# A list-scheduled recurrent scan on one Trainium2 core: loads on ScalarE's queue, state scaling on ScalarE, a fourth common bank, and new estimates

## The chip, the core and the metric

The kernel is one program on one core of a Trainium2 chip. Its engines are TensorE (PE, with its weight loads as PEld), VectorE (DVE), ScalarE (ACT), GpSimd (POOL) and SyncE (SP), which here only issues DMAs. Each runs its own instructions in order and they meet through semaphores. The metric is the device time of one execution in microseconds (us), lower is better. TensorE's clock has two levels, 1.2 and 2.4 GHz; the profile shows the granted clock as a share of the upper one.

## The reference

The model is a four-layer encoder on 528 tokens (16 meta tokens and 512 real ones) of 1024 features: latent attention (MLA) in layers 0 and 3, an RWKV-7 mixer in layer 1, a gated linear recurrence in layer 2, and a convolutional gated FFN behind each. The change is about the RWKV-7 mixer, 16 heads of 64 features in two directions:

```python
def _wkv7_scan(r, w, a, b, k, v, reverse):
    def step(S, inp):
        r_t, w_t, a_t, b_t, k_t, v_t = inp
        sa = jnp.einsum('bhvk,bhk->bhv', S, a_t)
        S = S * w_t[:, :, None, :] + sa[..., None] * b_t[:, :, None, :] + v_t[..., None] * k_t[:, :, None, :]
        return S, jnp.einsum('bhvk,bhk->bhv', S, r_t)
    ...
# in _rwkv7_mixer, for d in range(2):
    kd = kf * (1.0 + (a - 1.0) * k_a_h)
    ys.append(_wkv7_scan(rf, decay, -kk, kk * a, kd, vf, reverse=(d == 1)))
    bonuses.append(jnp.sum(rf * kd * r_k_h, axis=-1, keepdims=True) * vf)
```

Around it stand low-rank maps for decay, rate and gate, a normalisation of each head's output, and the output projection.

## The kernel before

The scan is computed in windows of 64 tokens. Eight pairs of heads times two directions make 16 chains; both heads of a pair lie side by side in the 128 partitions (64 each), so most matmuls are 64x64 and come in twos. What one chain i needs is written as Python generators that yield one operation at a time (`rwkv_scan`, from line 1362):

- `pair` loads r, k and v of a head pair (tiles `in_r`, `in_k`, `in_v`) from DRAM; `values` turns v.
- `stage_a` loads the second low-rank weights (`w2`), makes decay and rate, then the products `bk` and `xr`, and with matmuls `ps<-xr,bk` the masked matrices `am` (DVE).
- `inverses` inverts 16x16 diagonal blocks: SP sends blocks of `am` to DRAM (`sc<-am`) and loads them back one block per partition (`bu<-sc`); POOL does 15 elimination steps of two operations each (`dtmp<-bu,dt` and `dt<-dt,dtmp`); ACT copies the transpose (`dt<-dt`); SP sends it out and back (`sd<-dt`, `dc<-sd`, `xt<-sd`).
- `stage_b` builds the whole window inverse from it: DVE makes `dd<-dc`, then four products in a row, `rb<-dd,am`, `rb<-dd,nn` and twice `rb<-xt,nn`, each evicted by DVE before the next, and last `xa`.
- `chain` runs the nine windows one after another. In each, `ch<-s,xa` is copied by DVE to `u`, `ch<-u,tb` follows, and DVE's scalar_tensor_tensor makes the new state `s` from it and from `sp`, the old state times the decay. Before, `sp` is a POOL operation (line 1704). Chain i starts only when chain i-1 has ended.
- `bonus` and `post` finish a head pair; `post` loads the gate's weights (also a `w2` tile).

The order of all instructions is found at build time by the list scheduler `Streams`. `Op` estimates an operation's cost (and, for a DMA, a time `after` until the data are there); `LATENCY` adds a delay between engines; at each turn the operation that could start first by these estimates is emitted. Dependencies are kept on the chip by semaphores; a wrong estimate therefore only gives another order. The buffers set what may be ahead: three `am`, two `dc`, and a common set of PSUM banks (`ps`: three of the eight; two `ch`, one `rb`, one `yp`, one `idle`) that are taken and given back. Where the estimate leaves TensorE idle by over 150 ns and its estimated work of late is low, `fill` emits matmuls of 256 columns that nobody reads (fillers, "idle" in the rows). All operations of the scheduler are emitted at line 218, so rows are told apart by tiles. The MLA layers use the same class.

Of the kernel before, what the change touches and what calls it, by code (L numbers as in the profile page):

```python
# [48 lines left out]
GAP = 150.0  # L49
# [56 lines left out]
class Op:  # L106
    __slots__ = ("eng", "fn", "args", "kw", "outs", "ins", "cost", "work", "after", "mode")

    def __init__(self, eng, fn, name, args, kw):
        self.eng, self.fn, self.args, self.kw = eng, fn, args, kw  # L110
        aps = [x for x in list(args) + list(kw.values()) if hasattr(x, "tensor")]
        out = kw.get("out", args[0] if args else None)
        self.outs = [out] + ([kw["accum_out"]] if kw.get("accum_out") is not None else [])
        self.ins = [x for x in aps if all(x is not y for y in self.outs)]
        n = max([int(np.prod(x.shape[1:])) for x in aps if x is out or eng != "pe"] + [1])
        if eng == "pe":
            lhsT = kw.get("lhsT", args[1] if len(args) > 1 else None)
            m = lhsT.shape[-1]
            rows = lhsT.shape[0] / 128
            tile = lambda x: 32 if x <= 32 else 64 if x <= 64 else 128  # L120
            self.mode = tile(lhsT.shape[0]), tile(m)
            if lhsT.dtype == F32R:
                self.cost, self.work = max(2 * m, n) / 2.2, n * rows
            elif name == "transpose":
                self.cost, self.work = 2 * lhsT.shape[0] / 2.3, 2 * lhsT.shape[0] * rows
            else:
                self.cost, self.work = 4 * max(n, m / 2) * (0.56 if self.mode == (64, 64) else 0.35 if m <= 32 else 1.0) / 2.3, 4 * n * rows
        else:
            fixed, each = {"dve": (75, 0.5 if name == "tensor_scalar" else 1.04), "act": (50 if name == "copy" else 240 if kw.get("accum_out") is not None else 100, 0.835),
                           "pool": (140, 2.1), "dma": (475, 0)}[eng]  # L130
            self.cost = fixed + each * n
        self.after = 650 + 4 * out.shape[0] * n / 360 if eng == "dma" else 0.0


class Eng:
# [8 lines left out]
class Streams:  # L144
# [132 lines left out]
    def fill(self, start):  # L277

        t = self.free.get("pe", 0.0)
        self.did(t, 0.0)  # L280
        while start - t > GAP and self.work < NEED:
            n = max(64, min(256, int((start - t) * 2.4 * WARM))) // 2 * 2
            self.warm(n)
            t += n / 2.4
            self.did(t, n)
            self.mode = (128, 128)
        self.free["pe"] = t
# [38 lines left out]
class Kern:  # L326
# [1034 lines left out]
    def rwkv_scan(self, es, hid, rkv, yall):  # L1361
# [11 lines left out]
        def bank(name):  # L1373
            return sch.named(pp.tile([128, 512], F32, name=name, tag=name), name, 1)

        for kind, n in (("ps", 3), ("ch", 2), ("rb", 1), ("yp", 1)):
            for j in range(n):
                sch.slot(kind, lambda name=f"{kind}{j}": bank(name))
        sch.slot("sq", lambda: tl([128, T], "sq"))

        idle, dense = pp.tile([128, 512], F32, name="idle"), hid["w", 0]
        cst = cp.tile([128, a["rw_const"].shape[1]], F32, name="rwcst")
        nc.sync.dma_start(cst, a["rw_const"])
        mask = [cst[:, 128 * d:128 * d + 128] for d in range(2)]
# [82 lines left out]
        def pair(hp, P):  # L1467
            if hp >= 2:
                yield wait(f"bonus{hp - 2}")
            for n, name in ((2, "v"), (0, "r")):  # L1470
                P[name] = tl([128, T], "in_" + name, 2)
                yield dq.dma_start(P[name], rkv[n, hp])
            if hp >= 2:
                yield wait(f"front{2 * hp - 3}")
            P["k"] = tl([128, T], "in_k", 2)
            yield dq.dma_start(P["k"], rkv[1, hp])
            yield spawn(f"values{hp}", values(hp, P), prio("values", 2 * hp))
            kk = P["kk"] = tl([128, T], "kkh", 2)
            yield ve.tensor_scalar(out=kk, in0=P["k"], scalar1=self.p("rw_k_k", hp), scalar2=None, op0=ALU.mult)
            sq = yield take("sq")  # L1480
            yield ac.activation(out=sq, in_=kk, func=AF.Square)
            yield from over_norm(kk, sq, dict(scalar1=1e-24, scalar2=None, op0=ALU.max), dict(scalar1=0.5, scalar2=None, op0=ALU.mult))
            yield give(sq)
# [21 lines left out]
        def stage_a(i, hp, d, P, U):  # L1505
            if i:
                yield wait(f"front{i - 1}")
            if d == 0:
                raw = tl([128, 512], "w2")
                yield dq.dma_start(raw, a["rw_2"][hp, :, 0:512])  # L1510
                P["w2"] = tl([128, 512], "w2hi", 1, F32R), tl([128, 512], "w2lo", 1, F32R)
                yield from split(*P["w2"], raw)
            whi, wlo = P["w2"]
# [165 lines left out]
        def chain(i, hp, d, P, U):  # L1679
# [14 lines left out]
            for w, after in zip(order, order[1:] + [None]):  # L1694
# [5 lines left out]
                if after is not None:  # L1700
                    p1 = pc[:, w:w + 1]
                    if S is not None:
                        sp = tl([128, 64], "sp", 2)
                        yield po.tensor_tensor(out=sp, in0=S, in1=p1.to_broadcast([128, 64]), op=ALU.mult)
                    ps = yield take("ch")
                    yield from both(ps[:, 0:64], tb[:, 1, w], v[:, w], True, False)
                yield ve.tensor_copy(u[:, w], pu[:, 0:64])
# [42 lines left out]
        def post(hp, P):  # L1750
            yield wait(f"c{2 * hp + 1}", f"bonus{hp}", *([f"post{hp - 1}"] if hp else []))
            y = yall[:, hp]
            raw = tl([128, 512], "w2")[:, 0:256]
            yield dq.dma_start(raw, a["rw_2"][hp, :, 512:768])
            whi, wlo = tl([128, 256], "g2hi", 1, F32R), tl([128, 256], "g2lo", 1, F32R)
            yield from split(whi, wlo, raw)
            yield ac.copy(wlo[0:64, 128:256], whi[0:64, 128:256].bitcast(F32))
# [18 lines left out]
        for hp in range(KD):  # L1776
# [6 lines left out]
                sch.add(f"a{i}", stage_a(i, hp, d, P, U), prio("a", i))  # L1783
            sch.add(f"bonus{hp}", bonus(hp, P), prio("bonus", 2 * hp))
            sch.add(f"post{hp}", post(hp, P), prio("post", 2 * hp))
        sch.warm = lambda n: nc.tensor.matmul(idle[:, 0:n], lhsT=dense[:, 0:128], rhs=dense[:, 0:n], start=True, stop=True)
        with tc.manual_schedule():
            sch.run()
        if DEBUG:
# [144 lines left out]
```

## Time and profile before

| | us |
|---|---|
| median of three runs | 3481.4 (3481.07 to 3485.17) |
| profiled execution | 3473.31 |
| its span | 3471.5 |
| scan, from the first filler to the last DVE add of a chain | 992.6 to 1543.1 |
| ends of chains 4, 6, 8, 10 and 12 (copy of `yp`) | 1217.6, 1282.3, 1345.3, 1411.6, 1478.9 |

Over the span PE is busy 93%, DVE 78%, ACT 48% and POOL 27%. The steady part of the scan is best read between 1060 and 1480 us. There a matmul's busy time includes its way through the array, so two matmuls in a row overlap, and a busy PE isn't one that starts matmuls as fast as it could.

### The profile page before, as it was taken

Reading aid. Unit: us, or ns where it says so; the run is one execution under the profiler, and the core shown is the slowest. Engines: PE = TensorE matmul, PEld = TensorE weight load, DVE = VectorE, ACT = ScalarE, POOL = GpSimd, SP = SyncE. Lnnn points to the kernel's source line nnn. Section 1 sums busy time; section 2 is a strip of 40 time slices with the busy share of each in tenths; the row PEclk is TensorE's granted clock in tenths of the full one; section 3 lists DMA queues with packets and bytes.
Section 4 is the critical chain, followed back from the end, with each engine's and each line's share of the span. In section 5 each row is a group of like instructions: output and inputs, shape, how many; then the busy total and the mean of one; then the engine's idle time right before and its main releaser. Section 6 shows DMA issues by size and latency. Waiting matters only on the chain.

```text
span 3471.5 us, 77910 instructions
## 1 busy us (share of the span) xinstructions
PE 3216.4 (93%) x32057; PEld 3099.1 (89%) x32057; DVE 2701.7 (78%) x5006; ACT 1673.0 (48%) x3139; POOL 936.7 (27%) x1406
## 2 busy tenths in 40 slices
PE   7999999997988988879999988989999899989998
PEld 7899899996977878869999988989999799989998
DVE  6877789979336767657898788789886777788987
ACT  6665454433333333224544468654444666554443
POOL 0000143422016555433443200044331000034431
PEclk9999999998989999989999999999999999999999
DMA  2001223322322112113323222222322011112322
GB/s 84 34 33 40 84 71 104 99 87 88 136 69 50 35 40 45 25 42 102 98 95 107 80 73 74 80 73 88 106 86 83 21 38 35 65 64 83 101 93 72
DMA packets 157717, 250.07 MB, mean 72 GB/s; under 512 B 78736, under 2 KB 88112, under 8 KB 157232
## 3 DMA queue, kind: packets, MB, share of 16 engines
q1 hardware_dynamic: 157360, 245.08, 22.4%
q8 instruction: 252, 4.13, 0.5%
q14 instruction: 105, 0.86, 0.1%
HBM read 227.93 MB, written 17.10 MB: 71 GB/s over the span
## 4 chain that ended last, share of the span: by engine, by line
PE 47%; DVE 10%; ACT 6%; issue 2%; POOL 2%; DMA 2%; SPq 0%; DVEq 0%; ACTq 0%; POOLq 0%
PE bank L422 11%; PE bank L421 11%; PE bank L420 11%; PE pj L218 4%; PE ps L218 2%; PE s L218 1%; PE ch L218 1%; PE rb L218 1%; PE yp L218 1%; PE mm L420 1%; PE mm L421 1%; PE mm L422 1%; POOL dt L218 1%; ACT wv L218 1%; ACT th L1227 1%
## 5 line engine op out<-in xcount | busy, mean ns | idle before, releaser
L421 PE MATMUL bank<-xlo,whi 128*128 128x264 f32 x2272 | 655.7, 290 | 18.7 <-DVE xlo L562 10.9
L422 PE MATMUL bank<-xhi,wlo 128*128 128x264 f32 x2272 | 651.2, 289 | 12.4 <-DVE wlo L409 12.3
L420 PE MATMUL bank<-xhi,whi 128*128 128x264 f32 x2272 | 646.6, 289 | 15.4 <-ACT whi L408 13.8
L421 PEld LDWEIGHTS bank<-xlo,whi 128*128 128x128 f32 x2272 | 437.0, 192 | 26.1 <-DVE xlo L562 14.8
L420 PEld LDWEIGHTS bank<-xhi,whi 128*128 128x128 f32 x2272 | 432.7, 192 | 17.5 <-ACT whi L408 14.6
L422 PEld LDWEIGHTS bank<-xhi,wlo 128*128 128x128 f32 x2272 | 435.3, 192 | 14.4 <-DVE wlo L409 14.4
L422 PE MATMUL bank<-phi,wlo 128*128 128x264 f32 x1408 | 402.2, 286 | 0.0
L421 PE MATMUL bank<-plo,whi 128*128 128x264 f32 x1408 | 400.3, 284 | 0.0
L420 PE MATMUL bank<-phi,whi 128*128 128x264 f32 x1408 | 400.3, 284 | 0.0
L409 DVE TENSOR_TENSOR wlo<-wraw,whi 128x1024 fp32r<-128x1024 f32 (+1 forms) x234 | 262.8, 1125 | 116.0 <-ACT whi L408 115.8
L408 ACT CAST whi<-wraw 128x1024 fp32r<-128x1024 f32 (+1 forms) x234 | 222.4, 952 | 199.4 <-PE bank L421 157.8
L575 DVE TENSOR_TENSOR wlo<-wraw,whi 128x1024 fp32r<-128x1024 f32 (+1 forms) x216 | 286.3, 1326 | 29.7 <-ACT whi L574 28.1
L420 PEld LDWEIGHTS bank<-phi,whi 128*128 128x128 f32 x1408 | 265.4, 188 | 0.0
L422 PEld LDWEIGHTS bank<-phi,wlo 128*128 128x128 f32 x1408 | 264.9, 188 | 0.0
L421 PEld LDWEIGHTS bank<-plo,whi 128*128 128x128 f32 x1408 | 264.7, 188 | 0.0
L574 ACT CAST whi<-wraw 128x1024 fp32r<-128x1024 f32 (+1 forms) x216 | 195.2, 904 | 124.2 <-PE bank L421 72.4
L422 PE MATMUL bank<-thi,wlo 128*128 128x264 f32 x864 | 246.3, 285 | 0.0
L421 PE MATMUL bank<-tlo,whi 128*128 128x264 f32 x864 | 245.7, 284 | 0.0
L420 PE MATMUL bank<-thi,whi 128*128 128x264 f32 x864 | 244.9, 283 | 0.0
L589 POOL TENSOR_TENSOR wraw<-wraw,wsum 128x512 f32<-128x512 f32 x72 | 96.1, 1334 | 413.3 <-DVE wlo L575 368.2
L714 DVE SCALAR_TENSOR_TENSOR cv<-gp,par,cv 128x528 f32<-128x528 f32 x176 | 177.7, 1059 | 10.8 <-ACT cv L712 9.9
L422 PEld LDWEIGHTS bank<-thi,wlo 128*128 128x128 f32 x864 | 162.7, 188 | 0.4 <-DVE wlo L575 0.2
(403 smaller groups left out, 9708.2 us busy)
## 6 DMA issues: line engine op xcount, KB each, us to landing
wraw<-in_ffn_in_dram SPq DMA_DIRECT2D x176, 512.0 KB
wraw<-in_ffn_out_dram SPq DMA_DIRECT2D x96, 384.0 KB
wraw<-in_mla_o_dram SPq DMA_DIRECT2D x48, 256.0 KB
wraw<-in_rw_rkv_dram SPq DMA_DIRECT2D x24, 512.0 KB
wraw<-in_lru_in_dram SPq DMA_DIRECT2D x20, 512.0 KB
wraw<-in_mla_q_dram SPq DMA_DIRECT2D x16, 512.0 KB
wraw<-in_ffn_out_dram SPq DMA_DIRECT2D x16, 512.0 KB
rkv<-ro SPq DMA_DIRECT2D x24, 264.0 KB
```

The source lines that it names most:

```text
L218: op.fn(*op.args, **op.kw)
L408: nc.scalar.copy(hi[:, :cols], raw[:, :cols])
L409: nc.vector.tensor_tensor(out=lo[:, :cols], in0=raw[:, :cols], in1=hi[:, :cols].bitcast(F32), op=ALU.subtract)
L420: nc.tensor.matmul(out, lhsT=w[0][ws], rhs=x[0][xs], start=start, stop=False)
L421: nc.tensor.matmul(out, lhsT=w[0][ws], rhs=x[1][xs], start=False, stop=False)
L422: nc.tensor.matmul(out, lhsT=w[1][ws], rhs=x[0][xs], start=False, stop=stop)
L574: nc.scalar.copy(hi[:, cut], x[:, cut])
L575: nc.vector.tensor_tensor(out=lo[:, cut], in0=x[:, cut], in1=hi[:, cut].bitcast(F32), op=ALU.subtract)
L589: e.tensor_tensor(out=a1[:, 1], in0=a1[:, 1], in1=s[:, 1], op=ALU.subtract)
L714: nc.vector.scalar_tensor_tensor(out=c, in0=gp[:, q:q + T], scalar=self.p(f"fc_w{l}{q}", f), in1=c, op0=ALU.mult, op1=ALU.add)
L1227: nc.scalar.activation(out=self.two(v), in_=ps[:, :, :HT], func=AF.Tanh, scale=0.5, bias=z)
```

## The change

There are four parts. The loads of `in_v`, `in_r`, `in_k` and both `w2` tiles (40 DMAs) are issued on ACT instead of SP. `sp` is an ACT activation (Identity with a scale per partition) instead of a POOL operation. Fillers no longer have a bank of their own: each writes the first free bank of the common set, which now has four, and none is put where no bank is free. And the estimates are others: small fp32 matmuls in 64x64 mode count at least 64 columns, POOL counts 290 ns and 1.95 ns per column, and a DMA's data count as there 2 us (on ACT 3 us) after the issue instead of 650 ns.

```diff
--- before.py
+++ after.py
@@ -124,12 +124,12 @@
             elif name == "transpose":
                 self.cost, self.work = 2 * lhsT.shape[0] / 2.3, 2 * lhsT.shape[0] * rows
             else:
-                self.cost, self.work = 4 * max(n, m / 2) * (0.56 if self.mode == (64, 64) else 0.35 if m <= 32 else 1.0) / 2.3, 4 * n * rows
+                self.cost, self.work = 4 * max(n, m if self.mode == (64, 64) else m / 2) * (0.56 if self.mode == (64, 64) else 0.35 if m <= 32 else 1.0) / 2.3, 4 * n * rows
         else:
             fixed, each = {"dve": (75, 0.5 if name == "tensor_scalar" else 1.04), "act": (50 if name == "copy" else 240 if kw.get("accum_out") is not None else 100, 0.835),
-                           "pool": (140, 2.1), "dma": (475, 0)}[eng]
-            self.cost = fixed + each * n
-        self.after = 650 + 4 * out.shape[0] * n / 360 if eng == "dma" else 0.0
+                           "pool": (290, 1.95), "dma": (475, 0)}[eng]
+            self.cost = 150 if name == "dma_start" and eng == "act" else fixed + each * n
+        self.after = (2000 if eng == "dma" else 3000) + 4 * out.shape[0] * n / 360 if name == "dma_start" else 0.0
 
 
 class Eng:
@@ -278,9 +278,9 @@
 
         t = self.free.get("pe", 0.0)
         self.did(t, 0.0)
-        while start - t > GAP and self.work < NEED:
+        while start - t > GAP and self.work < NEED and self.slots["ps"]:
             n = max(64, min(256, int((start - t) * 2.4 * WARM))) // 2 * 2
-            self.warm(n)
+            self.warm(self.slots["ps"][0](), n)
             t += n / 2.4
             self.did(t, n)
             self.mode = (128, 128)
@@ -1373,12 +1373,12 @@
         def bank(name):
             return sch.named(pp.tile([128, 512], F32, name=name, tag=name), name, 1)
 
-        for kind, n in (("ps", 3), ("ch", 2), ("rb", 1), ("yp", 1)):
+        for kind, n in (("ps", 4), ("ch", 2), ("rb", 1), ("yp", 1)):
             for j in range(n):
                 sch.slot(kind, lambda name=f"{kind}{j}": bank(name))
         sch.slot("sq", lambda: tl([128, T], "sq"))
 
-        idle, dense = pp.tile([128, 512], F32, name="idle"), hid["w", 0]
+        dense = hid["w", 0]
         cst = cp.tile([128, a["rw_const"].shape[1]], F32, name="rwcst")
         nc.sync.dma_start(cst, a["rw_const"])
         mask = [cst[:, 128 * d:128 * d + 128] for d in range(2)]
@@ -1469,11 +1469,11 @@
                 yield wait(f"bonus{hp - 2}")
             for n, name in ((2, "v"), (0, "r")):
                 P[name] = tl([128, T], "in_" + name, 2)
-                yield dq.dma_start(P[name], rkv[n, hp])
+                yield ac.dma_start(P[name], rkv[n, hp])
             if hp >= 2:
                 yield wait(f"front{2 * hp - 3}")
             P["k"] = tl([128, T], "in_k", 2)
-            yield dq.dma_start(P["k"], rkv[1, hp])
+            yield ac.dma_start(P["k"], rkv[1, hp])
             yield spawn(f"values{hp}", values(hp, P), prio("values", 2 * hp))
             kk = P["kk"] = tl([128, T], "kkh", 2)
             yield ve.tensor_scalar(out=kk, in0=P["k"], scalar1=self.p("rw_k_k", hp), scalar2=None, op0=ALU.mult)
@@ -1507,7 +1507,7 @@
                 yield wait(f"front{i - 1}")
             if d == 0:
                 raw = tl([128, 512], "w2")
-                yield dq.dma_start(raw, a["rw_2"][hp, :, 0:512])
+                yield ac.dma_start(raw, a["rw_2"][hp, :, 0:512])
                 P["w2"] = tl([128, 512], "w2hi", 1, F32R), tl([128, 512], "w2lo", 1, F32R)
                 yield from split(*P["w2"], raw)
             whi, wlo = P["w2"]
@@ -1701,7 +1701,7 @@
                     p1 = pc[:, w:w + 1]
                     if S is not None:
                         sp = tl([128, 64], "sp", 2)
-                        yield po.tensor_tensor(out=sp, in0=S, in1=p1.to_broadcast([128, 64]), op=ALU.mult)
+                        yield ac.activation(out=sp, in_=S, func=AF.Identity, scale=p1)
                     ps = yield take("ch")
                     yield from both(ps[:, 0:64], tb[:, 1, w], v[:, w], True, False)
                 yield ve.tensor_copy(u[:, w], pu[:, 0:64])
@@ -1751,7 +1751,7 @@
             yield wait(f"c{2 * hp + 1}", f"bonus{hp}", *([f"post{hp - 1}"] if hp else []))
             y = yall[:, hp]
             raw = tl([128, 512], "w2")[:, 0:256]
-            yield dq.dma_start(raw, a["rw_2"][hp, :, 512:768])
+            yield ac.dma_start(raw, a["rw_2"][hp, :, 512:768])
             whi, wlo = tl([128, 256], "g2hi", 1, F32R), tl([128, 256], "g2lo", 1, F32R)
             yield from split(whi, wlo, raw)
             yield ac.copy(wlo[0:64, 128:256], whi[0:64, 128:256].bitcast(F32))
@@ -1783,7 +1783,7 @@
                 sch.add(f"a{i}", stage_a(i, hp, d, P, U), prio("a", i))
             sch.add(f"bonus{hp}", bonus(hp, P), prio("bonus", 2 * hp))
             sch.add(f"post{hp}", post(hp, P), prio("post", 2 * hp))
-        sch.warm = lambda n: nc.tensor.matmul(idle[:, 0:n], lhsT=dense[:, 0:128], rhs=dense[:, 0:n], start=True, stop=True)
+        sch.warm = lambda t, n: nc.tensor.matmul(t[:, 0:n], lhsT=dense[:, 0:128], rhs=dense[:, 0:n], start=True, stop=True)
         with tc.manual_schedule():
             sch.run()
         if DEBUG:
```

The order of instructions changes everywhere in the scan. On SP, at the end of the inverse of one chain and the beginning of the next (`sc` out and `bu` in, then `sd`, `dc` and `xt` of the result), the kernel before has

```order
L218 DMA sc_13457<-am_13266 16x16
L218 DMA bu_13477<-sc_13457 66x16x16
L218 DMA w2_13794<-in_rw_2_dram 128x512
L218 DMA sd_13846<-dt_13531 64x2x256
L218 DMA sd_13846<-dt_13531 2x256
L218 DMA dc_13856<-sd_13846 128x16x16
L218 DMA xt0_11290<-sd_13846 16x16 x2
L218 DMA sc_13904<-am_13792 64x8x64
L218 DMA sc_13904<-am_13792 16x16
```

and the changed one, at the same chains,

```order
L218 DMA sc_13387<-am_13281 16x16
L218 DMA bu_13504<-sc_13387 66x16x16
L218 DMA sc_13974<-am_13860 64x8x64
L218 DMA sc_13974<-am_13860 16x16
L218 DMA sc_13974<-am_13860 64x8x64
L218 DMA sc_13974<-am_13860 16x16
L218 DMA sd_14074<-dt_13581 64x2x256
L218 DMA sd_14074<-dt_13581 2x256
L218 DMA bu_14036<-sc_13974 66x16x16
```

The next chain's `sc` now stand ahead of `sd`, the previous result, and the `w2` load between them is gone from SP. On PE, in the last two products `rb<-xt,nn` of stage b of the eighth chain, the kernel before has the previous chain's matmuls (`ch`) between the pieces of the last one:

```order
L218 MATMUL ch0_15789<-s1_15814,xa_15360 64x64 x2
L218 MATMUL ch1_15828<-vt1_11289,tb_14511 64x64 x2
L218 MATMUL rb0_15800<-xt1_11291,nn_15564 64x16 x5
L218 MATMUL ps0_15819<-ident_65,bk0_11286 64x64 x2
L218 MATMUL rb0_15800<-xt1_11291,nn_15564 64x16 x5
L218 MATMUL ch1_15828<-u_15425,tb_14511 64x64 x2
L218 MATMUL ch0_15848<-r1_14513,xt0_11290 64x64 x2
L218 MATMUL rb0_15800<-xt1_11291,nn_15564 64x16 x3
```

In the changed kernel eleven fillers (`ps<-hid_w`, line 1786) stand between these two products; these are the last of them and what follows, with the semaphores that each waits for:

```order
L1786 MATMUL ps_16037<-hid_w_9624 128x256 [waits PE_49]
L1786 MATMUL ps_16039<-hid_w_9624 128x256 [waits PE_49]
L1786 MATMUL ps_16041<-hid_w_9624 128x256 [waits PE_49]
L1786 MATMUL ps_16043<-hid_w_9624 128x256 [waits PE_49]
L1786 MATMUL ps_16045<-hid_w_9624 128x256 [waits PE_49]
L218 MATMUL rb_16024<-xt_11290,nn 64x16 [waits DVE_49]
L1786 MATMUL ps_16048<-hid_w_9624 128x256 [waits PE_49]
L1786 MATMUL ps_16050<-hid_w_9624 128x256 [waits PE_49]
L218 MATMUL rb_16024<-xt_11290,nn 64x16 x9
L218 MATMUL ps_16063<-xr,bk_11286 64x128 [waits PE_49]
```

The previous chain's matmuls are gone from between, and each filler waits for PE's own semaphore: it is a tile of its own in the bank into which the filler before it wrote. The changed kernel has 134 fillers, 17 of them at the scan's start, where the kernel before has 41, 17 of them there. On ACT, in the middle of a chain, the state's scaling (`sp`) now stands among copies for other stages:

```order
L218 ACTIVATE sp_14064<-s1_14052,pc_12593 128x64
L218 COPY dt_13581<-dt_13581 66x256
L218 COPY tb_13975<-ps2_14058 128x64
L218 ACTIVATE sp_14100<-s1_14086,pc_12593 128x64
L218 COPY r1_13977<-ps3_13978 128x512
L218 ACTIVATE ta_13921<-ps1_13994,half_b_11297 128x264
L218 COPY dt_14114<-rwcst_11279 66x256
L218 ACTIVATE ta_13921<-ps3_14119,half_b_11297 128x264
L218 ACTIVATE ep_13919<-c_13918 128x528
```

The first `sp` here is followed by the copy of the finished inverse (`dt<-dt`), which needs POOL, before the next `sp`; that is so in 8 of the 96 places between two `sp` of one chain. In 48 of the 96 nothing stands between.

## Rows read from the trace of the kernel before

**Rows 1.** Busy time by engine in one stretch of the scan.

```profile
1060.00:1480.00 420.00, 370.63 (x8555) 338.93 (x8553) 287.11 (x758) 139.02 (x330) 224.33 (x567) 0.96 0.18 37
```

**Rows 2.** Chain of waits, 1060 to 1480 us, shares by line.

```profile
by line: PE ps L218 17.0%; PE ch L218 7.5%; PE rb L218 6.6%; POOL dt L218 5.4%; issue 5.2%; PE yp L218 5.0%; POOL dtmp L218 4.7%; DVE c L218 3.7%; DMA bu<-sc 3.6%; DMA sc<-am 3.4%; DVE am L218 3.0%; DVE xr L218 2.9%; DVE rs_t L218 2.4%; DMA
```

**Rows 3.** Waits of PE in the scan (us in total, times, longest us).

```profile
PE ch L218 <- DVE u L218: 11.4, 22, 3.6
PE ch L218 <- DVE s L218: 8.0, 10, 1.5
PE ps L218 <- DVE am L218: 7.7, 11, 1.9
PE rb L218 <- DVE xt L218: 7.6, 12, 1.2
...
PE rb L218 <- DVE dd L218: 2.5, 4, 0.8
```

**Rows 4.** Waits of ACT and POOL for the inverse in the scan.

```profile
ACT dt L218 <- POOL dt L218: 33.8, 14, 5.7
...
POOL dtmp L218 <- DMA bu<-sc: 23.3, 11, 7.0
```

**Rows 5.** Waits of the SP queue in the scan.

```profile
SPq L218 <- ACT dt L218: 165.2, 12, 21.0
```

**Rows 6.** SP in order of time: start us, us, issues.

```profile
1322.62 2.04 SPq L218 DMA_DIRECT2D xt<-sd  x2
1324.75 6.07 SPq L218 DMA_DIRECT2D sc<-am  x4
...
1352.36 1.08 SPq L218 DMA_DIRECT2D sd<-dt  x2
...
1355.28 1.45 SPq L218 DMA_DIRECT2D xt<-sd  x2
1356.76 0.58 SPq L218 DMA_DIRECT2D sc<-am  x1
```

**Rows 7.** Groups by form in the scan: busy us, mean ns.

```profile
L218 POOL TENSOR_TENSOR sp<-s,pc 128x64 f32<-128x64 f32 x112 | 38.0, 340 | 161.5 <-DVE s L218 159.6 <-DVE xr L218 1.4 <-DVE h L218 0.3
...
L218 ACT COPY r<-ps 128x64 f32<-128x64 f32 x16 | 3.4, 215 | 15.0 <-PE ps L218 15.0
```

**Rows 8.** DMA issues on SP: duration ns min/median/max.

```profile
L218 SPq DMA_DIRECT2D w<-in_rw_dram x16: 352/548/1523, 994.2 to 1512.8; - x16
...
L218 SPq DMA_DIRECT2D in_v<-rkv x8: 337/338/446, 994.7 to 1375.5; - x8
```

**Rows 9.** One step of the last chain, nothing beside it, in order of time.

```profile
1534.09 0.33 PE L218 MATMUL ch<-s,xa 64*64 64x64 f32 x4
1534.11 0.29 POOL L218 TENSOR_TENSOR sp<-s,pc 128x64 f32<-128x64 f32 x1 [1.15 <-DVE s L218]
...
1534.46 0.23 DVE L218 COPY u<-ch 128x64 f32<-128x64 f32 x1 [0.43 <-PE ch L218]
...
1534.74 0.33 PE L218 MATMUL ch<-u,tb 64*64 64x64 f32 x4 [0.21 <-DVE u L218]
...
1535.03 0.28 PE L218 MATMUL yp<-am,vt 64*64 64x64 f32 x4
...
1535.14 0.28 PE L218 MATMUL yp<-xr,s 64*64 64x64 f32 x4
1535.19 0.28 DVE L218 SCALAR_TENSOR_TENSOR s<-ch,pc,sp 128x64 f32<-128x64 f32 x1 [0.50 <-PE ch L218]
```

**Rows 10.** The first fillers, in order of time.

```profile
992.59 2.09 PEld L1786 LDWEIGHTS idle<-hid_w 128*128 128x128 f32 x17
992.71 2.18 PE L1786 MATMUL idle<-hid_w 128*128 128x256 f32 x17
```

**Rows 11.** Filler matmuls of the kernel before: ns min/median/max.

```profile
L1786 PE MATMUL idle<-hid_w x41: 274/283/583, 992.7 to 1546.8; 128*128 128x256 f32 x41
```

**Rows 12.** Busy tenths of PE in 40 slices of the span (the page).

```profile
PE   7999999997988988879999988989999899989998
```

## The prediction

> **What bounds the kernel now.** I first read the busy times of the scan, 1060 to 1480 us [rows 1]. PE is busy 370.6 of 420 us and no other engine over 287, but part of that is the way through the array. The chain of waits says what ends last [rows 2]: the largest part is PE's own products (`ps`, `ch`, `rb`, `yp`: 36.1%), then the inverse on POOL (`dt` and `dtmp`, 10.1% = 42.4 us) with its transfers (`bu<-sc` 3.6%, `sc<-am` 3.4%). The inverse as a whole holds 17.1%, or 71.8 us. PE's waits are many and short and nearly all for DVE [rows 3]: 11.4 us for `u`, 8.0 for `s`, 7.7 for `am`, 7.6 for `xt`. So no engine is full: an order, fixed beforehand, loses a little at each hop between PE and DVE, and more where the inverse is late. A chain alone has a period of 1.44 us a window, 13 us for nine [rows 9]; between the ends of chains 4 and 12 each took (1478.9 − 1217.6)/8 = 32.7 us. The recurrence alone is not the bound. The other views to see are ACT's and POOL's waits for the inverse [rows 4], SP's queue [rows 5] and SP in order of time [rows 6]: the next chain's `sc` starts at most 0.1 us after the last `xt` has been issued in 6 of the 15 places, so there SP, standing behind `sd`, which waits for ACT's copy, holds back the inverse that comes next.
>
> Outside the scan only the MLA layers' lists change. There PE's row is nearly all eights and nines [rows 12]; I put 0 on them, from −4 to +4.
>
> **The scaled state on ACT.** 112 POOL operations of 340 ns leave POOL [rows 7]. In the order 32 of them stand inside an inverse. These 32 × 0.34 = 10.9 us delay it; POOL's inverse is on the chain of waits for 42.4 of its 224.3 busy us, 19%, so −2.1 us. ACT gets 112 activations. Before shows none of that shape; the nearest rows are the copy of 128x64, 215 ns, and POOL's own 340 [rows 7]. Either fits: alone, `sp` ends at 1534.40 and is used at 1535.19, a slack of 0.79 us [rows 9], and ACT is busy 139 of 420. It costs something only where ACT waits for something else first: in 8 of 96 places the copy of the inverse stands ahead, and ACT's wait for POOL there was 33.8 us in 14 times, at most 5.7 [rows 4]. One place in two met, at 2.4 us less the slack, would be +6; but the list now knows better when POOL ends. I take 0, from 0 to +6.
>
> **Loads on ACT.** 40 DMAs leave SP, 338 to 548 ns each [rows 8], 14 to 22 us of issuing. SP had time (165 us of waits for ACT's copy alone [rows 5]), and what it gains is counted with the order below. On ACT, a third busy, the issues lie in gaps unless they wait for a free buffer with an `sp` behind; 4 of the 96 places have loads in them, 4 × 0.55 = 2.2 us, inside the slack. I take 0, from 0 to +3.
>
> **The fourth common bank.** What waits for a bank shows as `ps` standing late; PE's only wait of that kind is `ps<-am`, 7.7 us in 11 times [rows 3], in which a stage with three banks can't go ahead. I take all of it, −7.7; bounds 0 and −8.
>
> **The estimates.** A DMA's data now count as there after 2 us and not 0.65, and POOL's steps as longer, so the list lets more work go ahead of a late inverse: between a chain's `am` and its stage b, PE's matmuls in the order grow from about 22 to about 30 us of estimated work, and SP puts the next `sc` ahead of `sd` in 5 or 6 of the 15 places. The inverse then is late less often. What can be won is the 71.8 us that it holds; the least is nothing, and all of it, 71.8 less what POOL gets above and the bank's, some 64. I take a third, −24, since in 6 of 15 places SP is what holds the next inverse and the change undoes most of these (5.5/15 = 37%), and a place where the inverse is early has PE or DVE late next.
>
> Against it: the chain's hops have less beside them. With a product of both heads at 0.11 us (the two `yp` begin at 1535.03 and 1535.14), a hop PE–DVE–PE of about 0.65 us (`ch<-s,xa` begins at 1534.09, `ch<-u,tb` at 1534.74 [rows 9]) is covered by other matmuls in the order in 131 of 255 cases before and in 82 after; the sum of what is lacking grows by 14.8 us. Half of these hops stand where PE would have been late anyway; +7.4, from 0 to +15.
>
> **The fillers.** 24 stood after the scan's start and 117 do now. At the start they run freely, 17 in 2.18 us, 0.128 us each [rows 10]. The later ones of the changed kernel are different: every filler is a tile of its own and waits for PE's semaphore of the one before. A filler's record is 283 ns at the median [rows 11], LDWEIGHTS stands 0.12 us ahead of the matmul [rows 10], and a release takes 0.05 (DVE's `u` ends 1534.69, PE starts 1534.74 [rows 9]): at most 0.45 us a filler, where the list counts 256 columns at 2.4 GHz, 0.107. They fill places where PE would wait by the list, most in stage b's serial products, where PE then waited for DVE (7.6 us for `xt`, 2.5 for `dd` [rows 3]). Some is hidden, the rest pushes the next product back. The excess over the list's length is between 0 and 0.34 us; I take 0.14, two fifths, since the previous chain's `ch` are behind the fillers too: 117 × 0.14 = +16, from 0 to +40.
>
> The rule that speaks against this is in the Trainium skill, "TensorE: Matmul & The Clock Gate", "Part 2: What happens when you issue a matmul": a matmul hides the drain of the one before only in a stream, and one alone pays about 175 ns more than its columns. By it a filler that waits for the last would have an excess of 0.175, 117 × 0.175 = +20.5 us, an estimate from that page, and the forecast would be 3475.5. The trace's 283 ns [rows 11] agree with its 175 + 107 = 282.
>
> **Sum.** POOL −2.1, bank −7.7, inverse −24, hops +7.4, fillers +16, the rest 0: −10.4 us. The profiled execution took 3473.3 (3471.5 of span and 1.8 around it), so it would become 3462.9; it lies 8.1 below the median of the runs, 3481.4, which thus becomes **3471.0**. The forecast's own range is 3458 (the inverse's term half again as large) to 3474 (the end of what counts as faster, below).
>
> **Rivals.**
> - *The serial fillers decide (slower).* Place: stage b's four products, where up to eleven fillers stand between two. At the full excess 0.34 they cost +40 instead of +16: −10.4 + 24 = +13.6, 3495. It decides from an excess on the path of 26.4/117 = 0.23 us a filler. For it: the chain's matmuls are behind them, and PE's products are the largest part of the chain of waits [rows 2]. Against: PE waited there anyway [rows 3].
> - *The inverse was late only in name (no change).* What was behind it is late next, and the gain is half of what I take, −12: +1.6, 3483. For it: PE waits for DVE in every row [rows 3], and POOL's waits for `bu<-sc` are 23.3 us in all [rows 4].
> - *The fillers hold the clock (faster).* The granted clock is 0.96 between 1060 and 1480 us [rows 1]. Between the levels 1 and 0.5 that is 8% of the time at the lower one, 34 us, which at the upper would take 17 less: −27, 3454. For it: 117 fillers stand where PE is idle. Against: products in stage b fill few columns, and hops between PE and DVE don't shorten with the clock. The Trainium skill says in the same page, "Part 1: The HAM clock gate", that the throttled state is the default and activity releases it; by that rule fillers of 256 columns in idle places would be what lifts 0.96, and this rival gets its chance from the row, not from the page.
> That the order changes and no wait does, so that the change doesn't do what it says, is part of the second.
>
> **How the numbers follow.** 0.2%, 7 us, is about what a measurement can tell from no change. Chances: forecast 0.31, clock 0.18, no change 0.17, slower 0.34. Faster thus 0.49, same 0.17, slower 0.34. For 8 in 10 the range goes from 3436 (the clock's case, 3454, with the inverse's gain at −42 of the −64 that its bound allows) to 3502 (the slower case with the hops at their +15).
>
> **What would show it.** Right or wrong by step: POOL without `sp` and its inverse share of the chain of waits below 17.1% (if not, the inverse's −24 is wrong); `SPq<-ACT dt` smaller and `sc` well ahead of `sd`; PE's wait `ps<-am` gone (the bank); ACT's `sp` at 215 to 340 ns and DVE's `s` never waiting for ACT (else +6); the fillers' distance when they stand in a row, 0.13 or 0.45 us, and waits of PE for itself ahead of `ps<-hid_w`; granted clock from 1060 to 1480 above 0.96 (the clock). The forecast is wrong if the ends of chains 4 and 12 are not closer than 261 us, or if the MLA stages have moved by more than 4 us.

## The result, and the profile after

The changed kernel takes 3561.5 us (median of 4 runs, 3556.6 to 3562.0) against 3481.2 before: ratio 1.0221, 95% interval 1.0208 to 1.0234, 80 us slower, where 3471 was forecast and the range ended at 3502. The profiled execution has a span of 3559.9 us, 88.4 more than before. Nearly all of it is in the scan: its last DVE add of a chain ends at 1628.8 us and not at 1543.1 (85.7 us later), though its first filler matmul starts at 991.4 and not at 992.7; what stands behind the scan takes 2.7 us more. The ends of chains 4 and 12 (1255.8 and 1536.9 us) are 281.1 us apart, 261.3 before.

The same stretch as in [rows 1], and 20 us of it apart (columns as there):

```profile
1060.00:1480.00 420.00, 369.78 (x7258) 322.70 (x7256) 250.81 (x651) 140.76 (x356) 173.19 (x421) 0.86 0.16 33
1072.00:1092.00 20.00, 18.35 (x150) 12.70 (x152) 2.10 (x5) 0.93 (x2) 10.75 (x37) 0.50 0.10 14
```

PE is as busy as before, with 7258 matmuls for 8555; on the mean each takes longer. The granted clock is 0.86, not 0.96, and in the 20 us it is at the lower level throughout, with PE "busy" 18.35 us on 150 matmuls. The chain of waits of the same 420 us, for [rows 2]:

```profile
by line: PE ps L218 34.2%; PE rb L218 11.2%; PE ch L218 10.5%; PE ps L1786 7.9%; PE yp L218 6.0%; DVE xr L218 4.0%; issue 2.7%; DVE xt L218 2.5%; DVE rs_y L218 1.8%; DVE bk L218 1.6%; DMA sd<-dt 1.6%; DVE rs_t L218 1.5%; DMA dc<-sd 1.5%; DV
```

No step of the inverse on POOL is left in it, as the change wants. What stands there instead is PE, 69.8% for 36.1, with the fillers (`ps L1786`) at 7.9%. Waits of the whole scan, 992 to 1640 us, for [rows 3, 4] (us in all, times, longest):

```profile
ACT xa L218 <- PE ps L218: 112.8, 16, 19.3
...
POOL dtmp L218 <- ACT dt L218: 96.7, 6, 22.9
...
PEld ps L1786 <- PE ps L1786: 34.5, 105, 0.4
POOL dtmp L218 <- DMA bu<-sc: 32.2, 3, 19.2
...
PE rb L218 <- DVE xt L218: 23.9, 18, 6.2
...
PE ch L218 <- DVE u L218: 12.0, 35, 1.6
ACT dt L218 <- POOL dt L218: 11.5, 2, 10.0
...
DVE s L218 <- ACT sp L218: 1.8, 2, 1.1
...
PE ps L218 <- DVE am L218: 0.7, 1, 0.7
```

and two of the kernel before that stand beside them:

```profile
ACT xa L218 <- PE ps L218: 15.5, 11, 4.0
...
DVE s L218 <- POOL sp L218: 6.0, 5, 2.6
```

`ps<-am` fell from 7.7 to 0.7, ACT's wait for POOL's `dt` from 33.8 to 11.5, and DVE's wait for `sp` from 6.0 to 1.8: three things that the change removes are nearly gone. POOL's wait for `bu<-sc` did not fall, 32.2 us for 23.3. New are fillers that wait for a filler, 34.5 us in 105 times, and `rb<-xt` went up to 23.9 us from 7.6. ACT's `xa`, the last of stage b, waits 112.8 us for PE and not 15.5, and POOL 96.7 us for a `dt` copy of ACT, which had no such row before.

The first stage b of the scan shows best what the fillers do. PE in order of time (start us, us, what), where [rows 10] had fillers 0.128 us apart:

```profile
1069.19 1.97 PE L218 MATMUL rb<-dd,am 64*64 64x64 f32 x32 [5.02 <-DVE dd L218]
1071.09 5.70 PE L1786 MATMUL ps<-hid_w 128*128 128x256 f32 x9
1076.72 1.97 PE L218 MATMUL rb<-dd,nn 64*64 64x64 f32 x32
1079.48 1.92 PE L218 MATMUL rb<-xt,nn 64*64 64x32 f32 x32 [0.79 <-DVE xt L218]
1081.33 3.14 PE L1786 MATMUL ps<-hid_w 128*128 128x256 f32 x5
1084.40 0.39 PE L218 MATMUL rb<-xt,nn 64*64 64x16 f32 x2
1084.73 1.22 PE L1786 MATMUL ps<-hid_w 128*128 128x256 f32 x2
1085.88 1.89 PE L218 MATMUL rb<-xt,nn 64*64 64x16 f32 x30
1087.69 2.50 PE L1786 MATMUL ps<-hid_w 128*128 128x256 f32 x4
1090.12 2.19 PE L218 MATMUL ps<-xt,at 64*64 64x64 f32 x36
```

and the DVE copy for which the second product needs to wait, and the filler loads behind one another:

```profile
1071.21 0.69 DVE L218 TENSOR_TENSOR nn<-rb,rwcst 128x512 f32<-128x512 f32 x1 [1.35 <-PE rb L218]
```
```profile
1071.72 0.29 PEld L1786 LDWEIGHTS ps<-hid_w 128*128 128x128 f32 x1 [0.35 <-PE ps L1786]
1072.36 0.29 PEld L1786 LDWEIGHTS ps<-hid_w 128*128 128x128 f32 x1 [0.35 <-PE ps L1786]
```

`nn` is ready at 1071.90, and `rb<-dd,nn` starts at 1076.72: nine fillers, 0.64 us apart, hold it up by 4.8 us. The whole stage b, 21 us, is five products and 20 fillers. As that of the first chain it has no previous chain to stand beside it in either kernel. Before, its first four products took 7.8 us (from 1063.4) at the granted clock 1.00, with matmuls `ps<-ident,bk` and `ps<-vt,am` between them; here they take 18.6 us at 0.50. Over the kernel (for [rows 11]; ns min/median/max) most fillers run at the lower level:

```profile
L1786 PE MATMUL ps<-hid_w x134: 279/582/583, 991.4 to 1635.4; 128*128 128x256 f32 x134
```

The scaled state and a load on ACT, for [rows 7, 8]: `sp` has a mean of 347 ns, and the issue of a weight load a median of 339 ns on ACT, where it had 548 on SP:

```profile
L218 ACT ACTIVATE sp<-s,pc 128x64 f32<-128x64 f32 x112 | 38.9, 347 | 90.5 <-DVE s L218 90.1
```
```profile
L218 ACTq DMA_DIRECT2D w<-in_rw_dram x16: 334/339/442, 991.7 to 1625.6; - x16
```

SP's wait for ACT's copy of the inverse, for [rows 5], did not shrink; it is 30% of the scan as before, so the next `sc` ahead of `sd` shows no gain there:

```profile
SPq L218 <- ACT dt L218: 192.1, 12, 29.3
```

### The profile page after: what moved, and what is told of

The parts are those of the page before. It is cut to its first block, busy times and chain, and to the rows that moved or that the text cites. A ratio compares the mean times of both kernels' runs of the same rounds, so it can differ in the third digit from the quotient of the medians.

```text
span 3559.9 us, 78021 instructions
## 1 busy us (share of the span) xinstructions
PE 3300.8 (93%) x32150; PEld 3147.5 (88%) x32150; DVE 2709.3 (76%) x5006; ACT 1707.6 (48%) x3251; POOL 905.1 (25%) x1294
## 4 chain that ended last, share of the span: by engine, by line
PE 73%; DVE 14%; ACT 8%; issue 3%; DMA 1%; POOL 0%; ACTq 0%; SPq 0%; DVEq 0%; POOLq 0%
PE bank L422 16%; PE bank L421 15%; PE bank L420 15%; PE pj L218 8%; PE ps L218 6%; PE s L218 3%; PE ch L218 2%; PE ps L1786 2%; PE rb L218 2%; PE yp L218 1%; ACT wv L218 1%; ACT p L218 1%; DVE pst L218 1%; PE mm L422 1%; PE mm L421 1%
## 5 line engine op out<-in xcount | busy, mean ns | idle before, releaser
L421 PE MATMUL bank<-xlo,whi 128*128 128x264 f32 x2272 | 653.8, 289 | 19.4 <-DVE xlo L562 11.5
L422 PE MATMUL bank<-xhi,wlo 128*128 128x264 f32 x2272 | 648.9, 288 | 13.4 <-DVE wlo L409 13.4
L420 PE MATMUL bank<-xhi,whi 128*128 128x264 f32 x2272 | 644.9, 289 | 17.1 <-ACT whi L408 15.5
L421 PEld LDWEIGHTS bank<-xlo,whi 128*128 128x128 f32 x2272 | 435.0, 191 | 27.5 <-DVE xlo L562 15.5
L420 PEld LDWEIGHTS bank<-xhi,whi 128*128 128x128 f32 x2272 | 430.5, 191 | 19.6 <-ACT whi L408 16.6
L422 PEld LDWEIGHTS bank<-xhi,wlo 128*128 128x128 f32 x2272 | 433.3, 191 | 15.5 <-DVE wlo L409 15.5
```

The source lines that it names most:

```text
L420: nc.tensor.matmul(out, lhsT=w[0][ws], rhs=x[0][xs], start=start, stop=False)
L421: nc.tensor.matmul(out, lhsT=w[0][ws], rhs=x[1][xs], start=False, stop=False)
L422: nc.tensor.matmul(out, lhsT=w[1][ws], rhs=x[0][xs], start=False, stop=stop)
```

## The experiments

Ratios are to the kernel before on the same chip, with their 95% intervals; 0.1% is 3.5 us. One count goes beside them, from the program's order and not from a trace: how many matmuls of the previous chain (`ch`, `yp`) stand between the first and the last product of a stage b (the one for `xa`), on the mean of 16 (74.5 before, 51.1 in the changed kernel).

**The fillers.** In `a_share` the order is that of the changed kernel; in `a_nofill` there are no fillers, and all else stands in the order of the changed kernel too.

```diff
+        tile = None
         while start - t > GAP and self.work < NEED and self.slots["ps"]:
-            self.warm(self.slots["ps"][0](), n)
+            tile = self.slots["ps"][0]() if tile is None else tile
+            self.warm(tile, n)
# a_nofill
-        while start - t > GAP and self.work < NEED and self.slots["ps"]:
+        while start - t > GAP and self.work < 0 and self.slots["ps"]:
```

> The changed kernel in the same order, but the fillers of one gap write one tile, so that only the first of a gap waits for an earlier tile. Theory F (the fillers' own waits are the loss: in the changed kernel 9 in a row took 5.70 us, 0.63 each, where the order counts 0.107): some 100 fillers get 0.4 us shorter, 3515 to 3530. Theory O (the new estimates make a bad order, the fillers only stand where PE would wait): 3550 to 3565.

> The changed kernel without any filler (the list is made again without them). F: 3490 or less, since all of 134 x 0.53 us = 72 us of PE's time goes. O: 3540 to 3570, since the hops that the fillers filled stay; then the granted clock of the scan is below the 0.86 of the changed kernel.

Measured: `a_share` 3515.6 us, 1.0089 (1.0074 to 1.0104); `a_nofill` 3510.9, 1.0077 (1.0062 to 1.0092). The fillers' waits for each other cost 1.3%, 46 us, with no other instruction moved, as F expected; but without any filler 0.8% is left, where F had nothing left and O all of it, so neither theory alone gives the time. The stage b above, in `a_share` (the whole of it is 13 us for 21):

```profile
1070.40 2.29 PE L1788 MATMUL ps<-hid_w 128*128 128x256 f32 x9
1072.61 1.97 PE L218 MATMUL rb<-dd,nn 64*64 64x64 f32 x32
```

Its granted clock from 1060 to 1480 us is 0.92. The same stage in `a_nofill`, also at 0.50 throughout:

```profile
1064.28 1.97 PE L218 MATMUL rb<-dd,am 64*64 64x64 f32 x32 [4.29 <-DVE dd L218]
1067.04 1.97 PE L218 MATMUL rb<-dd,nn 64*64 64x64 f32 x32 [0.79 <-DVE nn L218]
1069.81 1.92 PE L218 MATMUL rb<-xt,nn 64*64 64x32 f32 x32 [0.79 <-DVE xt L218]
1072.79 1.89 PE L218 MATMUL rb<-xt,nn 64*64 64x16 f32 x32 [1.06 <-DVE xt L218]
```

The first four products take 10.4 us there, so the waits that the fillers were to fill are 0.8 to 1.1 us each. The granted clock from 1060 to 1480 us is 0.89 without fillers, and not below the changed kernel's 0.86 as O expected.

**The estimates, together and apart.** `b_est` is the kernel before with all of them, `a_noest` the changed kernel with the old ones; `b_aft`, `b_mm` and `b_pool` have one each.

```diff
# b_est: all three;  b_mm, b_pool, b_aft: one each
-   4 * max(n, m / 2) * (0.56 ...
+   4 * max(n, m if self.mode == (64, 64) else m / 2) * (0.56 ...
-   "pool": (140, 2.1)
+   "pool": (290, 1.95)
-   self.after = 650 + ...
+   self.after = (2000 if eng == "dma" else 3000) + ...
```

> The kernel before with the new estimates alone: fillers in their own bank, 145 of them, sp on POOL, loads on SP. F: 3480 to 3500, the fillers are many but run freely (0.13 us each). O: 3540 or more.

> The changed kernel with the estimates of before (small matmuls, POOL and DMA; only the loads issued on ACT count as they count on SP before): 47 fillers. F: 3475 to 3490, only 6 fillers more than before, with waits of their own. O: 3470 to 3485. It tells whether the three other parts cost anything by themselves.

> The kernel before with one estimate changed: a DMA's data count as there 2 us after the issue, not 650 ns. Theory D (this one lets work for the next chain go ahead of a late inverse and leaves stage b and the chain without cover): most of the 38 us of the three estimates together, 3505 to 3525. Theory P (POOL's steps, 15 in a row at 290 ns instead of 140, lengthen the inverse in the list more than any DMA does): 3480 to 3495.

> The kernel before with one estimate changed: small fp32 matmuls count at least 64 columns. D and P: within 10 us of the kernel before. Theory M (stage b's last products, 16 columns each, count twice as long and their evictions come late in the list): 3500 or more.

> The kernel before with one estimate changed: POOL counts 290 ns + 1.95 ns a column, not 140 + 2.1. P: 3505 to 3525, since the inverse gets 30 x 0.14 = 4 us longer in the list and its data are later by that than by the DMA's estimate of three hops. D: 3480 to 3495.

| | us | ratio | interval | count |
|---|---|---|---|---|
| b_est | 3522.7 | 1.0109 | 1.0094 to 1.0125 | 45 |
| a_noest | 3499.6 | 1.0049 | 1.0032 to 1.0066 | 75 |
| b_aft | 3490.2 | 1.0016 | 1.0006 to 1.0025 | 56 |
| b_mm | 3481.8 | 0.9996 | 0.9985 to 1.0008 | 69 |
| b_pool | 3528.4 | 1.0126 | 1.0111 to 1.0140 | 56 |

The estimates alone cost 1.1% with 145 fillers in a bank of their own, whose records have a median of 283 ns. Of the three numbers it is POOL's: theories D and M fall, and P is right about which, at 3 us beyond its range. `b_est` lies between what F and O expected: its fillers run freely, so the order costs more than F allowed, and less than O. `a_noest` is above both: the other three parts cost 0.5% by themselves (below). `b_pool`'s chain of waits has the same turn from POOL to PE as the changed kernel:

```profile
by line: PE ps L218 31.5%; PE ch L218 9.1%; PE rb L218 8.7%; DMA dc<-sd 5.0%; PE yp L218 4.6%; issue 3.4%; DVE xr L218 3.4%; DMA sd<-dt 3.2%; DMA sc<-am 3.0%; PE idle L1786 2.7%; DVE xt L218 2.7%; DMA bu<-sc 2.7%; DMA in_k<-rkv 2.1%; DVE c 
```

**POOL's number.** `a_pool0` is the changed kernel with POOL's old estimate, `a_pool0share` the same with shared filler tiles; `b_p0` and `b_p215` are the kernel before with other values.

```diff
-   "pool": (290, 1.95)
+   "pool": (140, 2.1)       # a_pool0, a_pool0share
-   "pool": (140, 2.1)
+   "pool": (75, 1.04)       # b_p0;   (215, 2.0) in b_p215
```

> The changed kernel with POOL's old estimate alone (140 + 2.1 a column). Its order has 67 matmuls of the previous chain beside stage b on average (changed kernel 51, before 74.5), and 113 fillers. Theory P (POOL's estimate takes the previous chain away from beside stage b, and that is most of what the estimates cost): 3500 to 3530, the rest being fillers that wait for each other. Rival (in the changed kernel the DMA's 2 us do the same alone): 3545 or more.

> The kernel before with POOL counted still faster than it is, 75 + 1.04 a column: 82 matmuls of the previous chain beside stage b. P, carried on: the time goes on falling, 3460 to 3478. Rival (PE and ACT then stand in order and wait for an inverse that is late, and there is a best value near the old one): 3485 to 3510, with ACT's wait for POOL's dt above the 34 us of before.

> The kernel before with POOL counted as 215 + 2.0 a column, half way to the new estimate: 66 matmuls of the previous chain beside stage b (74.5 before, 56 at the new one). Theory P with a best value between (75 + 1.04 took 3533, 140 + 2.1 3482, 290 + 1.95 3528): 3488 to 3515, between the two. Rival (any other order than the one that was tuned is some 40 us worse, the number itself means nothing): 3520 or more, or 3482 or less.

> The changed kernel with POOL's old estimate and with fillers that share one tile a gap: the two causes undone together. If they add (46 for the fillers' waits in the changed kernel at 117 of them, here 96; 44 for POOL's estimate): 3475 to 3490. If they are one thing (the fillers stand where POOL's estimate put them): 3505 to 3517.

| | us | ratio | interval | count |
|---|---|---|---|---|
| a_pool0 | 3517.3 | 1.0106 | 1.0091 to 1.0121 | 67 |
| b_p0 | 3532.6 | 1.0139 | 1.0124 to 1.0154 | 82 |
| b_p215 | 3504.2 | 1.0059 | 1.0044 to 1.0073 | 66 |
| a_pool0share | 3488.8 | 1.0020 | 1.0011 to 1.0029 | 67 |

From the old value the time rises either way: 1.4% at 75 + 1.04, 0.6% half way to the new one, 1.3% there. That P carried on would gain is refuted by `b_p0`, 23 us beyond the rival's range as well, and its chain of waits shows what stands there: PE and ACT stand in their order and wait for an inverse that is late, 24.3% on POOL for 10.1 in [rows 2], and ACT's wait for POOL's `dt` went from 33.8 to 54.8 us, as the rival expected.

```profile
by line: PE ps L218 15.7%; POOL dt L218 12.4%; POOL dtmp L218 11.9%; issue 8.6%; DMA w<-in_rw_dram 5.2%; DMA sc<-am 4.2%; DMA dc<-sd 4.2%; DMA bu<-sc 3.6%; PE ch L218 3.4%; DVE am L218 3.4%; PE rb L218 3.1%; SPq L218 2.9%; DVE dd L218 2.1%;
```

`a_pool0` and `b_p215` fall where P put them. With POOL's old estimate and shared tiles 0.2% of 2.2% is left, so the rest of the estimates, `sp`, the loads and the bank together come to 7 us there. The two causes add but overlap: POOL's estimate is worth 1.15% with fillers that wait and 0.69% with ones that don't, the waits 1.32% and 0.86%. Of the 117 fillers behind the start 96 are left with the old estimate, so some of them stand where the new one put them.

**The scaled state, the loads, the bank.** `b_sp`, `b_ld` and `b_bank` are the kernel before with one part of the change; `b_bankshare` has the bank with shared tiles and `b_bsmm` the matmuls' estimate with it. In `o_both` and `o_ld` the list counts as before, so that PE's and DVE's orders stay:

```diff
# o_both; o_ld has the loads alone
-   yield po.tensor_tensor(out=sp, in0=S, in1=p1.to_broadcast([128, 64]), op=ALU.mult)
+   yield Op("pool", nc.scalar.activation, "activation", (), dict(out=sp, in_=S, func=AF.Identity, scale=p1))
-   yield dq.dma_start(P[name], rkv[n, hp])
+   yield Op("dma", nc.scalar.dma_start, "dma_start", (P[name], rkv[n, hp]), {})
...
```

> The kernel before with the scaled state on ACT alone. Of the 15 us that the three parts cost with the old estimates: theory S (sp waits behind ACT's in-order waits, DVE's new state behind it) 3490 to 3500; the rival (sp costs nothing, as its slack of 0.79 us says; the 15 us are the loads' or the bank's) 3478 to 3486.

> The kernel before with the 40 loads on ACT alone, old estimates. The three parts together cost 15 us, sp alone 3. Theory L (the loads on ACT are what is left): 3490 to 3497. Rival (they cost nothing, it is the bank's fillers): 3478 to 3487.

> The kernel before with four common banks and the fillers in them alone: 53 fillers, 36 of them after the start, that wait for each other. By the 46 us that sharing a tile gave back for 117 such fillers, 36 cost some 14 us: 3488 to 3500, less what the fourth bank gives. Rival (the fourth bank gives 7.7 us as I forecast and the few fillers stand where PE waits anyway): 3470 to 3482.

> The kernel before with four common banks, the fillers of one gap sharing one tile. With a tile each it took 3487. If its fillers' waits cost anything: 3478 to 3484; if the 5 us are the list's other order: 3485 to 3490.

> The kernel before with sp and the 40 loads on ACT, but in the order of before: the list still counts sp as POOL's and the loads as SP's, so PE's and DVE's orders are word for word those of before. Theory R (what sp and the loads cost by themselves, 3 and 10 us, comes from the list's other order, not from ACT): 3474 to 3486. Rival A (ACT's queue is where they lose, behind its in-order waits): 3490 or more.

> The order of before with only the 40 loads on ACT, sp on POOL. sp and loads together in that order took 8 us more. Rival A by the loads (ACT issues them just before it needs them: its waits for the low-rank weights, 14.2 us in 5 times before, were 27.9 in 15 with both moved): 3488 to 3496. A by sp: 3480 to 3485.

> The kernel before with four common banks, shared filler tiles and the new cost of small matmuls: 85 matmuls of the previous chain beside stage b, more than in any order so far but with POOL as before. Theory P with a best value between: more cover at an inverse estimate that holds, 3470 to 3479. Rival (too much stands behind a late inverse, as at POOL's 75 + 1.04): 3485 or more.

| | us | ratio | interval |
|---|---|---|---|
| b_sp | 3488.0 | 1.0012 | 1.0001 to 1.0023 |
| b_ld | 3492.2 | 1.0031 | 1.0022 to 1.0040 |
| b_bank | 3487.4 | 1.0011 | 1.0001 to 1.0022 |
| b_bankshare | 3478.5 | 0.9989 | 0.9979 to 0.9998 |
| o_both | 3492.0 | 1.0024 | 1.0011 to 1.0037 |
| o_ld | 3498.7 | 1.0042 | 1.0028 to 1.0056 |
| b_bsmm | 3490.4 | 1.0024 | 1.0011 to 1.0036 |

The loads alone cost 0.3 to 0.4%, and that with PE's order unchanged too (0.2% there together with `sp`): not the list's other order (theory R) but ACT's queue is where they lose. `o_ld` is 3 us beyond its range. ACT issues `w2` just ahead of the copy that needs it, and then waits for the data: from the issue to the start of that copy the median of the 16 weight loads is 7.1 us before and 2.7 in `o_ld`. The waits in `o_ld`, and behind it in the kernel before:

```profile
ACT w2hi L218 <- DMA w<-in_rw_dram: 16.6, 8, 2.8
ACT g2hi L218 <- DMA w<-in_rw_dram: 13.6, 7, 3.2
```
```profile
ACT w2hi L218 <- DMA w<-in_rw_dram: 11.5, 3, 6.0
...
ACT g2hi L218 <- DMA w<-in_rw_dram: 2.7, 2, 1.5
```

In all 30.2 us for 14.2. In the changed kernel, whose list counts 3 us for a load on ACT, the same two rows come to 13.4 us (8.6 and 4.8), no more than before; what the loads cost in it was not measured by itself. `sp` alone (`b_sp`) is 0.1%, between the ranges of theory S and of its rival, and lies at the edge of what can be told; that `o_both` is not slower than `o_ld` says that `sp` costs nothing by itself. Fillers that wait, 36 of them after the start, make the difference between `b_bank` and `b_bankshare`, 0.2%, and the fourth bank then gains 0.1%: `b_bankshare` is the one version that beats both kernels, though by less than 0.2%. More cover by the matmuls' estimate on top of it (`b_bsmm`, count 85) loses it again, as the rival there expected.

## Why the prediction was wrong

Two places of the sum carry the miss. The estimates, forecast at −16.6 us (inverse −24 and hops +7.4), measured +38 in `b_est`; the fillers, forecast at +16, measured +46 in `a_share`.

- **The fillers (+16, to +40 at most).** This term failed, in the place that the slower rival named and at over its price: 46 us by `a_share`. The excess was bounded at 0.34 us from rows at the upper clock: 0.12 + 0.283 + 0.05. There the rows after have 0.44 us a filler (loads start at 992.22, 992.66, ...), as bounded; but most ran at the lower level, 0.64 us apart, an excess of 0.53 over the list's 0.107. The longer one was to be seen: [rows 11] gives 283 ns as the median and 583 as the largest. The 175 ns that the Trainium skill gives a matmul that can't hide its drain ("TensorE: Matmul & The Clock Gate", "Part 2: What happens when you issue a matmul") fell short as well: the trace has the next weight load waiting too, 0.35 us of wait and 0.29 of load at the lower level.
- **The clock (rival, −27).** It went the other way, 0.96 to 0.86. In the stage b shown the clock fell to the lower level between 1066 and 1068 us, after PE had been idle since 1064.2 for `dd`, and 20 fillers with the products between them did not bring it back by 1092; it was back at 1096, when matmuls of the next stage ran close together. The same stage b without fillers is at the lower level too (`a_nofill`). At the scan's start it even fell from 1.00 to 0.50 at about 996 us while fillers 0.44 us apart were running.
- **The inverse (−24).** The mechanism was right as far as it goes, POOL is off the chain of waits; the gain is not there. I took work that goes ahead of a late inverse as a gain and its absence later as a small price. As the orders read, it is the same work: what the list puts ahead of stage b no longer stands beside it (51.1 matmuls for 74.5), and the steps that wait for DVE there run bare. The bound given as 64 us is 62 by its own terms, and the lower end given as 3458 is 3459; neither decides anything.
- **The hops (+7.4, to +15).** That price, mis-sized: the estimates alone cost 38 us net of all gain (`b_est`), POOL's number 44 by itself. Counting only hops without cover left out the clock. From the first to the last `rb` product the granted clock is 1.00 in 15 of the 16 stages b before (0.91 in the other); in the changed kernel it is below 0.90 in eight, seven of which have fewer than 45 matmuls of the previous chain beside them, and 1.00 in all five that have 86 or more. With the same order and no fillers (`a_nofill`) it is still below 0.90 in six. Two stages do not fit (68 beside it at 0.69, 18 at 1.00). At the lower level a product takes nearly twice as long (the 32 `rb<-xt,nn` of 16 columns 1.89 us in the row of `a_nofill`, 1.11 in the same stage before).
- **Loads on ACT (0, to +3).** 11 to 15 us with the old estimates (`b_ld`, `o_ld`). I priced the issues and their slot before `sp`, and not that ACT issues a load behind its earlier copies, 2.7 us ahead of its own reader and not 7.1. With the new estimates ACT's waits for the weights did not grow, so this term may have held in the changed kernel.
- **`sp` on ACT, and POOL's relief (0 and −2.1).** Within what can be told: 0.1%. I read a slack of 0.79 us from one step [rows 9] and passed over DVE's wait for POOL's `sp`, 6.0 us in 5 times, of which 1.8 are left on ACT.
- **The bank (−7.7).** The wait `ps<-am` did go (7.7 to 0.7 us); by itself, with shared tiles (`b_bankshare`, where 2.7 us of that wait are left), the bank is worth about half, 0.11% = 4 us.
- **MLA (0 ± 4).** Right: 2.7 us more behind the scan, 1.3 less ahead of it.

What stays open: no single count of the order gives the time. `b_aft` has as little cover as `b_pool` (56), and costs 0.16% and not 1.26%; `b_bsmm` has the most and is slower than `b_bankshare`. That the loss of cover, with the clock that goes with it, is what POOL's estimate costs is read from the orders, the chains of waits and the clock of the stages; no run changes the cover alone, so it is argued and not shown.

## What to carry to other kernels

An estimate in a greedy list scheduler is a setting and not a measurement. Here the nearly true duration of POOL's steps (0.38 to 0.40 us apart on the chip at 63 columns; the new number says 0.41, the old 0.27) gave an order 1.3% worse than the wrong one, and a number still smaller 1.4%. Work that fills waiting time must not wait for itself; give one tile to a run of fillers, and bound its price by the rows at the lower clock. A load is better on a queue that is free early than on that of the engine that reads it, where the list doesn't allow for its landing: here that cost 0.3 to 0.4%.

## What the runs showed of the hardware

Fillers of 256 columns that wait for each other neither brought the clock back nor held it in the two places shown: PE was busy 92% of the time between 1072 and 1092 us at the granted clock 0.50, and at the scan's start it fell while they ran. With the same fillers sharing a tile (0.25 us apart in the row above, at the lower level too) the clock of the same stage b rose to 0.84 between 1074 and 1076 us and was back at 0.50 between 1080 and 1084; the mean clock from 1060 to 1480 us was 0.92 instead of 0.86, and with no filler at all (`a_nofill`) 0.89, in the same time (ratios 1.0089 and 1.0077, whose intervals overlap): here the higher clock that fillers gave paid for no more than their own time.
